# Five per-token rows sent through DRAM, one transposition for the stabiliser, the last token tile in two halves, and another order of the first loads

## The chip, the cores and the metric

The kernel runs on one core of a Trainium2 chip. The metric is the time of one launch on the device in microseconds (us); of several launches the median is given.

## The reference, cut to what matters

One layer of a streaming encoder over 2048 tokens of 1024 features, all in float32:

```python
xn = rms_norm(x, mix_norm_g)
aq, ak, av, mq, mk, mv, mo, i, f, ga, gm = split(xn @ w_in)
A = chunk_band_attention(aq, ak, av, rel_bias)      # chunks of 64 and 8 chunks before them
M = sigmoid(mo) * rms_norm(mlstm_chunkwise(silu(conv(mq, mk)), mv, i, f), mh_norm_g)
y = sigmoid(ga) * (A @ w_att_proj) + sigmoid(gm) * (M @ w_mlstm_proj)
x = x + y @ w_out
x = x + square(relu(rms_norm(x, ffn_norm_g) @ w_up)) @ w_down
return rms_norm(x, final_norm_g)
```

In `mlstm_chunkwise` each token and head has a stabiliser `m_t`, the running maximum that is subtracted before an exponential is taken. Each `rms_norm` needs one factor per token, `(mean of squares + eps) ** -0.5`.

## The kernel before, in words

**Tiles.** The 2048 tokens are four blocks of 512 (`T`). Activations mostly lie with the features on the 128 partitions and 512 tokens along the free side, so a factor per token has to be a row of 512 numbers that is the same on every partition. Where such a factor is computed, it lies the other way round: a tile of 128 partitions by 4 columns, token `t * 128 + p` at partition `p`, column `t`.

**Products.** Every large product is made of float32 tiles that are split in a rounded high part (a copy to fp32r on ScalarE, line 585) and the rest as a low part (a subtraction on VectorE, line 587). Three matmuls with 512 columns replace one: high by high, high by low, low by high. Blocks of 2 by 2 such products are done as seven products of sums, the sums being prepared by VectorE and ScalarE and partly kept in DRAM. Weights come from DRAM on SyncE's queue in tiles of 512 KB into four buffers (`wraw`), split into three (`wsplit`), and TensorE takes them in a fixed sequence.

**The order of the work.** The program first plays through itself in a planner (`Flow`): each step is a generator that yields an engine and a cost in nanoseconds (`yield "pe", 1080`), a wait for an event, or a buffer from a pool. The planner has a clock per engine, adds latencies between engines, lets an event carry the time at which it is set, and gives out the instructions in the order in which they start in its model. A first pass finds how late each step may be, and the second takes the order from these due times. `!` behind an engine's name puts a step first, and `~` marks short float32 work for TensorE. The framework below then schedules anew by priority. On VectorE and ScalarE only the callback `near` (lines 2841 to 2851) binds it: an instruction may not go ahead of those that the planner placed over 10 us (VectorE) or 6 us (ScalarE) earlier. Each engine then works its instructions off in order.

**The places that the change touches.**

- *Start* (`split_first` 553, `loader` 451, `square_in` 1362, `setup` 362). Ten small matmuls run at once (line 370). The first weight tile is loaded in two halves; both are rounded on ScalarE (568) and their rest is taken on VectorE (570). The eight tiles of `x` of block 0 are loaded in turn with the first four weight tiles: events `x_sent` and `w_sent` say which load waits for which in the planner. Each `x` tile is scaled and rounded (1374, ScalarE), its rest taken (1376, VectorE), squared (1383) and summed (1387).
- *Rows* (`rows_far` 1342, `final_scale` 2666). A factor of 128 by 4 becomes a row on all partitions by four matmuls with the identity: the column, repeated 128 times, is the weight. A copy on ScalarE takes the row out of PSUM. `rows_far(0)` does it for blocks 0 and 1, `rows_far(1)` for blocks 2 and 3, and `final_scale` for blocks 0, 1 and 2 at the final norm.
- *Stabiliser* (`gates_rest` 1720). For each of the four blocks the tile `mt` (128 tokens by 16, four groups of tokens times four heads) is turned by four transpositions of 128 by 4, copied out as 4 by 512 and stored to DRAM (`mtd`), from where `load_rec` reads one head's row to all partitions.
- *Last block* (`turned` 2508, `turn_part`, `down_turned` 998, `turned_out` 2562, `turned_put` 2590). The last product of block 3 is made with the tokens on the partitions: four token tiles of 128, each a PSUM bank of 512 features, c = 0 to 3 being the parts of the sum. For c = 3 the tiles are finished one after the other, 12 matmuls each. Behind each tile follow an addition (2570) and a product with the gain (2574) on VectorE, the square with its sum (2586) on ScalarE, a small sum (2577), the power -0.5 on GpSimd (2579), the scaling of two halves of the features (2596, 2599) and two stores, one issued by SyncE (2607) and one by ScalarE (2604). `turned` prepares `eps` times the squared norm of the middle from the row `midd` in DRAM: a square on ScalarE, then four matmuls with a column of ones (2522).

Of the kernel before, what the change touches and what calls it, by code (L numbers as in the profile page):

```python
# [26 lines left out]
ALU = mybir.AluOpType  # L27

P = 128
# [103 lines left out]
class Flow:  # L133
# [32 lines left out]

    def set(self, ev):
        ev.at = self.now
        ev.by = tuple(self.cur.by)
# [144 lines left out]
class Layer:  # L314
    LATE, LANDED = 4000.0, 10000.0

    def __init__(self, nc, pool, psum, io, due=None):
        self.nc, self.io = nc, io
        self.fl = Flow(due)
        self.make_tiles(pool, psum)  # L320
# [130 lines left out]
    def loader(self):  # L451
        fl, io = self.fl, self.io
        i = 0
        for kind, n in self.weights():
# [98 lines left out]
    def split_first(self, src, raw, sent):  # L553

        fl, nc = self.fl, self.nc
        w = yield from self.slot_w(0)
        self.wtile[0] = w
        evs = [Event(), Event()]
        for k, ev in enumerate(evs):
            yield "sp", 800, 2000  # L560
            nc.sync.dma_start(raw[:, k * 512:k * 512 + 512], src[:, k * 512:k * 512 + 512])
            fl.set(ev)
# [435 lines left out]
    def down_turned(self, s, m, ring, A, aev):  # L998
# [3 lines left out]
        for c in range(4):  # L1002
            ws = []
            steps = [(kk, t) for kk in range(2) for t in range(NT)]
            for kk, t in steps if c < 3 else sorted(steps, key=lambda x: x[1]):
# [4 lines left out]
                wv = ws[kk].rearrange("p a (q k n) -> p a k q n", q=2, k=2)  # L1010
                ps = bank[t].rearrange("p (q n) -> p q n", q=2)
                for k in range(2):
                    yield "wait", [aev[m, c][2 * kk + k]]
                    yield "pe", 681
                    a = A[m, c, 2 * kk + k][:, :, t * P:(t + 1) * P]
                    for x, y in ((0, 0), (1, 0), (0, 1)):
                        mm(ps, a[:, y], wv[:, x, k], start=c == kk == k == x == y == 0,  # L1017
                           stop=c == 3 and kk == k == y == 1)
                if kk == 1 and c == 3:
                    fl.spawn(self.turned_out(t, bank[t]), 1)  # L1020
                if t == NT - 1 and c < 3:
                    fl.put(self.wsplit, ws[kk])
            fl.put(ring, *[A[m, c, k] for k in range(4)])

# [317 lines left out]
    def rows_far(self, s, ready, read):  # L1342
# [4 lines left out]
        for b in range(2):  # L1347
            yield "wait", [self.ev_r[2 * s + b]]
            (bk,) = yield "get", self.banks, 1
            yield "pe", 1080  # L1350
# [9 lines left out]
        fl.put(self.bias, *got)  # L1360

    def square_in(self, b, k, x, tot, ev):

        fl, nc = self.fl, self.nc
        dst, g = self.blk[b]["xg"][k], self.gcol[:, 0, k:k + 1]
        if b == 0 and k > 0:
            yield "wait", [self.w_sent[(k - 1) // 2]]
        yield "sp", 800, 2000
        nc.sync.dma_start(x[:, :T], self.io["xt"][b, k])
        if b == 0:  # L1370
            fl.set(self.x_sent[k])
        yield "wait", [self.ev_gain]
# [347 lines left out]
    def gates_rest(self, b, bk):  # L1720
# [82 lines left out]
        V.tensor_scalar(ex[:, 2], ex[:, 2], C1, None, op0=ALU.mult)  # L1803
        yield "pe~", 428
        for c in range(NT):
            nc.tensor.transpose(bk[:MH, c * P:(c + 1) * P], sm["mt"][:, c * MH:(c + 1) * MH], self.ident)
        (tmp,) = yield "get", self.temp, 1
        yield "act", act_ns(512, True)
        nc.scalar.copy(tmp[:MH, :512], bk[:MH])
        fl.put(self.banks, bk)  # L1810
        fl.set(B["gates"])
        fl.spawn(self.store(self.mtd.ap()[b], tmp[:MH, :512], B["rows"], self.temp, tmp), 1)

# [666 lines left out]
    def final(self, s):  # L2480
        fl = self.fl
        tot, mid = yield "get", self.bias, 2
        fl.spawn(self.turned(s, mid), 2)
        summed, ready, sent = [Event() for _ in range(KT + 1)], Event(), []
# [22 lines left out]

    def turned(self, s, mid):

# [5 lines left out]
        for o in range(2):  # L2515
            nc.sync.dma_start(self.tgain[o], self.io["grow"][:, o * 512:o * 512 + 512].to_broadcast([P, 512]))
        ev = Event()
        yield from self.final_mid(2 * s + 1, mid[:, :512], ev)
        (bk,) = yield "get", self.banks, 1
        yield "pe~", 900  # L2520
        for t in range(NT):
            nc.tensor.matmul(bk[:, 2 * t:2 * t + 2], mid[:, t * P:(t + 1) * P], self.ones, start=True, stop=True)
        r, sums = self.rr["z3"], self.rq
        yield "dve", 150
        V.tensor_scalar(r, bk[:, :2 * NT].rearrange("p (t a) -> p t a", a=2)[:, :, 0], 1.0 / D, None, op0=ALU.mult)
        fl.put(self.banks, bk)
        fl.put(self.bias, mid)
        done = [Event() for _ in range(2 * NT)]
# [33 lines left out]
    def turned_out(self, t, ps):  # L2562
# [16 lines left out]
        nc.gpsimd.tensor_tensor(r, r, self.half[:, :1], op=ALU.pow)  # L2579
        fl.spawn(self.turned_put(t, 1, r), 1)  # L2580
        fl.spawn(self.turned_put(t, 0, r), 1)

    def turned_square(self, ps, sums, ev):
        (sq,) = yield "get", self.temp, 1
        yield "act", act_ns(512, True, 1)
        self.nc.scalar.activation(sq[:, :512], ps, AF.Square, accum_out=sums)
        self.fl.put(self.temp, sq)
        self.fl.set(ev)

    def turned_put(self, t, o, r):  # L2590

        nc = self.nc
        x = self.tout[t, o]
        if o or t < NT - 1:
            yield "act", act_ns(512, False, 1)
            nc.scalar.mul(x, x, r)
        else:
            yield "dve", dve_ns(512)
# [67 lines left out]
    def final_scale(self, s, h, slot, summed, ready):  # L2666
# [12 lines left out]
        nc.gpsimd.tensor_tensor(r, r, self.half, op=ALU.pow)  # L2679
        (bk,) = yield "get", self.banks, 1  # L2680
        yield "pe~", 1080
        for t in range(NT):
            nc.tensor.matmul(bk[:, t * P:(t + 1) * P], r[:, t:t + 1].to_broadcast([P, P]), self.ident,
                             start=True, stop=True)
        yield "act", act_ns(512, True)
        nc.scalar.copy(slot[:, :512], bk)
        fl.put(self.banks, bk)
        fl.set(ready)
# [13 lines left out]
    def build(self):  # L2702
# [15 lines left out]
        self.gated, self.mtd = f32d("gatepart", 40, T), f32d("mrow", NB, MH, T)  # L2718
        self.rbd = f32d("relrow", AH, 512)
        self.fin_ev = [E(KT) for _ in range(2)]  # L2720
        self.fin = [f32d(f"fin{h}", KT, P, T) for h in range(2)]
# [139 lines left out]
```

## Time and profile before

| | us |
|---|---|
| median of 3 runs | 2727.39 (2727.08 to 2732.34) |
| span of the profiled execution, first to last instruction | 2725.8 |
| TensorE busy in it | 2708.3 (99%), 12784 matmul records |
| VectorE busy | 2108.8 (77%) |
| ScalarE busy | 1542.1 (57%) |
| GpSimd busy | 48.0 (2%) |

The span is the only time that the profile gives for its own execution; the median lies 1.6 us above it. Each float32 matmul with the identity or with ones leaves two records, a transposition and an fp32r matmul leave one. "PE" is the matmul side of TensorE and "PEld" its weight loads. The rows of a timeline read: start, how long the merged run lasted, engine, line, operation, output and inputs, shapes, how many; in brackets the engine's idle time before it and what ended that.

### The profile page before, as it was taken

Reading aid. Unit: us, or ns where it says so; the run is one execution under the profiler, and the core shown is the slowest. Engines: PE = TensorE matmul, PEld = TensorE weight load, DVE = VectorE, ACT = ScalarE, POOL = GpSimd, SP = SyncE. Lnnn points to the kernel's source line nnn. Section 1 sums busy time; section 2 is a strip of 40 time slices with the busy share of each in tenths; the row PEclk is TensorE's granted clock in tenths of the full one; section 3 lists DMA queues with packets and bytes.
Section 4 is the critical chain, followed back from the end, with each engine's and each line's share of the span. In section 5 each row is a group of like instructions: output and inputs, shape, how many; then the busy total and the mean of one; then the engine's idle time right before and its main releaser. Section 6 shows DMA issues by size and latency. Waiting matters only on the chain.

```text
span 2725.8 us, 38104 instructions
## 1 busy us (share of the span) xinstructions
PE 2708.3 (99%) x12784; PEld 2253.3 (83%) x12784; DVE 2108.8 (77%) x3750; ACT 1542.1 (57%) x2685; POOL 48.0 (2%) x79
## 2 busy tenths in 40 slices
PE   9999999999999999999999999999999999999998
PEld 8878888888888887888888888888888888888887
DVE  7878876888877879987768888889798665657675
ACT  6545456776753645566556766656345565554443
POOL 0000000000000000000000000000000000000000
PEclk9999999999999999999999999999999999999999
DMA  8777889888877889867779787776864454578773
GB/s 305 275 258 277 301 286 293 272 242 275 262 234 238 270 302 321 286 214 265 266 236 288 244 257 225 240 232 220 276 227 160 163 197 159 189 271 285 274 239 134
DMA packets 336712, 678.29 MB, mean 249 GB/s; under 512 B 37396, under 2 KB 66708, under 8 KB 336516
## 3 DMA queue, kind: packets, MB, share of 16 engines
q1 hardware_dynamic: 335796, 674.80, 74.1%
q8 instruction: 100, 1.64, 0.3%
q10 hardware_dynamic: 720, 1.06, 0.1%
q14 instruction: 96, 0.79, 0.1%
HBM read 458.27 MB, written 214.30 MB: 247 GB/s over the span
## 4 chain that ended last, share of the span: by engine, by line
PE 86%; DVE 7%; DMA 3%; issue 2%; ACT 2%; SPq 0%; POOL 0%; ACTq 0%; POOLq 0%; DVEq 0%
PE bank L715 34%; PE bank L746 11%; PE bank L647 8%; PE bank L648 8%; PE bank L646 8%; PE bank L1181 3%; PE bank L751 2%; PE bank L1550 2%; PE bank L1625 2%; PE bank L1657 2%; DVE wsp L587 1%; PE bank L1017 1%; DMA tmp<-in_x 1%; DMA x<-ctx 1%; PE bank L1885 0%
## 5 line engine op out<-in xcount | busy, mean ns | idle before, releaser
L715 PE MATMUL bank<-r,wsp 128*128 128x512 f32 x4872 | 1111.3, 390 | 2.2 <-DVE ctx L2086 1.1
L715 PEld LDWEIGHTS bank<-r,wsp 128*128 128x128 f32 x4872 | 913.0, 188 | 195.0 <-DVE ctx L2086 3.5
L585 ACT CAST wsp<-wraw 128x1024 fp32r<-128x1024 f32 x437 | 459.1, 1051 | 491.4 <-PE bank L715 167.8
L587 DVE TENSOR_TENSOR wsp<-wraw,wsp 128x1024 fp32r<-128x1024 f32 x437 | 534.0, 1222 | 239.0 <-ACT wsp L585 233.7
L646 PE MATMUL bank<-r,wsp 128*128 128x512 f32 x960 | 379.3, 395 | 0.0
L648 PE MATMUL bank<-r,wsp 128*128 128x512 f32 x960 | 375.3, 391 | 0.0
L647 PE MATMUL bank<-r,wsp 128*128 128x512 f32 x960 | 375.2, 391 | 0.0
L746 PE MATMUL bank<-r,wsp 128*128 128x512 f32 x1512 | 368.6, 394 | 0.9 <-DVE ctx L941 0.7
L746 PEld LDWEIGHTS bank<-r,wsp 128*128 128x128 f32 x1512 | 279.0, 188 | 56.9 <-DVE ctx L941 1.6
L648 PEld LDWEIGHTS bank<-r,wsp 128*128 128x128 f32 x960 | 180.2, 188 | 38.5
L647 PEld LDWEIGHTS bank<-r,wsp 128*128 128x128 f32 x960 | 180.5, 188 | 33.4
L646 PEld LDWEIGHTS bank<-r,wsp 128*128 128x128 f32 x960 | 180.4, 188 | 33.5
L1398 DVE TENSOR_TENSOR r<-r 128x512 fp32r<-128x512 f32 x255 | 167.9, 684 | 20.6 <-ACT r L1393 20.0
L2086 DVE TENSOR_TENSOR ctx<-bank,ctx 128x512 f32<-128x512 f32 x174 | 118.9, 686 | 70.3 <-PE bank L715 67.5
L1393 ACT CAST r<-r 128x512 fp32r<-128x512 f32 x255 | 148.8, 617 | 33.4 <-DMA r<-u 30.4
L604 DVE TENSOR_TENSOR wraw<-wraw,wraw 128x1024 f32<-128x1024 f32 x112 | 136.4, 1218 | 4.3 <-DMA wsum<-wraw 3.3
L1638 ACT ACTIVATE sc<-sc,scs 128x640 f32<-128x640 f32 (+4 forms) x128 | 97.6, 763 | 67.5 <-DVE scs L1631 66.5
L2078 ACT COPY ctx<-bank 128x512 f32<-128x512 f32 x174 | 100.9, 583 | 61.0 <-PE bank L715 43.4
L2407 ACT ACTIVATE ctx<-ctx 128x512 f32<-128x512 f32 x96 | 60.6, 631 | 103.2 <-DVE ctx L2086 103.1
L1662 DVE TENSOR_TENSOR r<-bank,r 128x512 fp32r<-128x512 f32 (+1 forms) x168 | 95.7, 593 | 15.0 <-ACT r L1660 14.4
L1550 PE MATMUL bank<-r,r 128*128 128x512 f32 x336 | 94.8, 364 | 0.0
L1660 ACT CAST r<-bank 128x512 fp32r<-128x512 f32 (+1 forms) x168 | 81.0, 516 | 17.2 <-PE bank L1657 16.0
(267 smaller groups left out, 3253.3 us busy)
## 6 DMA issues: line engine op xcount, KB each, us to landing
wraw<-in_wf SPq DMA_DIRECT2D x196, 512.0 KB, 4.9
r<-u SPq DMA_DIRECT2D x224, 256.0 KB, 4.3
wraw<-wsum SPq DMA_DIRECT2D x104, 512.0 KB, 4.6
u<-ctx SPq DMA_DIRECT2D x128, 256.0 KB, 2.4
ctx<-in_wf SPq DMA_DIRECT2D x104, 256.0 KB, 4.4
wsum<-ctx SPq DMA_DIRECT2D x104, 256.0 KB, 4.2
u<-tmp SPq DMA_DIRECT2D x96, 256.0 KB, 2.7
ctx<-in_xt SPq DMA_DIRECT2D x64, 256.0 KB, 4.8
```

What stands on the lines that cost most here:

```text
L585: nc.scalar.copy(w[:, 0], raw)
L587: nc.vector.tensor_sub(w[:, 1], raw, w[:, 0].bitcast(F32))
L604: V.tensor_sub(dst, x, y)
L646: mm(ps, lh, rh, start=first, stop=False)
L647: mm(ps, lh, rl, start=False, stop=False)
L648: mm(ps, ll, rh, start=False, stop=last)
L715: mm(ps, wv[:, x, k, n], a[:, y], start=new and k == 0 and x == y == 0, stop=k == 3 and x == 1, skip_group_check=True)
L746: mm(ps, wv[:, x, k, n], a[:, y], start=start and x == y == 0, stop=stop and x == 1, skip_group_check=True)
L1393: self.nc.scalar.copy(dst[:, 0], src)
L1398: self.nc.vector.tensor_sub(dst[:, 1], src, dst[:, 0].bitcast(F32))
L1550: nc.tensor.matmul(bkv[:, :, c0:c0 + w], st, sl[:, :, o:o + w], start=n == 0, stop=n == total - 1)
L2086: nc.vector.tensor_add(t[:, o:o + 512], ps, t[:, o:o + 512])
```

## The change

Rows: `rows_far(1)` and `final_scale` (five rows in all) store the factor of 128 by 4 to a row of 512 in DRAM, wait for that store, and read the row back to all 128 partitions. `rows_far(0)` stays. `turned` reads one row of `midd` as 128 by 4 and squares it on VectorE, in place of the whole tile, its square and the matmuls.

Stabiliser: one transposition of 128 by 16, one copy of 16 by 128, and a store that puts the 16 rows in place.

Last token tile: for c = 3 the fourth tile is made in two halves of 256 features, 24 matmuls, each half followed by its own addition, square and product. For the other three tiles the product with the gain and the scaling become one VectorE instruction that reads PSUM; the third tile's waits until the fourth's sum is there.

Start: the first half of the first weight tile is rounded on VectorE. The weight tiles are let in one `x` tile earlier, `x` tile `k` now waits for `w_sent[k // 2]`, and some events carry other times. For the planner's first 12 us, and from c = 3 of the last product on (`strict`), VectorE and ScalarE follow the planner's order exactly.

```diff
-    def set(self, ev):
-        ev.at = self.now
+    def set(self, ev, early=0.0):
+        ev.at = (self.now[0] - early, self.now[1])
...
-                yield "wait", [self.x_sent[2 * i]]
+                yield "wait", [self.x_sent[max(0, 2 * i - 1)]]
...
         if sent is not None:
-            self.fl.set(sent)
+            self.fl.set(sent, 2000)
...
         for k in range(2):
             c = slice(k * 512, k * 512 + 512)
             yield "wait", [evs[k]]
-            yield "act", act_ns(512)
-            nc.scalar.copy(w[:, 0, c], raw[:, c])
+            if k == 0:
+                yield "dve!", dve2_ns(512)
+                nc.vector.tensor_copy(w[:, 0, c], raw[:, c])
+            else:
+                yield "act", act_ns(512)
+                nc.scalar.copy(w[:, 0, c], raw[:, c])
...
+            if c == 3:
+                self.strict = True
+                half, self.last_ev = Event(), Event()
+                for q in range(2):
+                    for kk in range(2):
+                        for k in range(2):
+                            yield "pe", 341
...
+                            for x, y in ((0, 0), (1, 0), (0, 1)):
+                                mm(bank[-1][:, q * 256:q * 256 + 256], a[:, y], wv[:, x, k, q], start=False,
+                                   stop=kk == k == y == 1, skip_group_check=True)
+                    fl.spawn(self.turned_half(q, bank[-1], half), 1)
...
+            if s == 1:
+                yield from self.row_of(self.rin[2 + b], self.rowd.ap()[b:b + 1], got[b][:, :T])
+                self.rows[b] = got[b][:, :T]
+                continue
...
+    def row_of(self, r, row, to):
+        kept = Event()
+        yield from self.store(row.rearrange("o (t p) -> p (o t)", p=P), r, kept)
+        yield "wait", [kept]
+        yield "sp", 800, 2500
+        self.nc.sync.dma_start(to, row.to_broadcast([P, T]))
...
         if b == 0 and k > 0:
-            yield "wait", [self.w_sent[(k - 1) // 2]]
-        yield "sp", 800, 2000
+            yield "wait", [self.w_sent[k // 2], self.x_sent[k - 1]]
+        land = 2000 if b else 2650
+        yield "sp", 800, land
...
-        yield "pe~", 428
-        for c in range(NT):
-            nc.tensor.transpose(bk[:MH, c * P:(c + 1) * P], sm["mt"][:, c * MH:(c + 1) * MH], self.ident)
+        yield "pe~", 107
+        nc.tensor.transpose(bk[:16, 0:P], sm["mt"], self.ident)
...
-        ev = Event()
-        yield from self.final_mid(2 * s + 1, mid[:, :512], ev)
-        (bk,) = yield "get", self.banks, 1
-        yield "pe~", 900
-        for t in range(NT):
-            nc.tensor.matmul(bk[:, 2 * t:2 * t + 2], mid[:, t * P:(t + 1) * P], self.ones, start=True, stop=True)
...
+        nc.sync.dma_start(r, self.midd.ap()[2 * s + 1, 0].rearrange("(t p) -> p t", p=P))
         yield "dve", 150
+        V.scalar_tensor_tensor(r, r, EPS, r, op0=ALU.mult, op1=ALU.mult)
...
-        yield "dve", dve_ns(512)
-        V.tensor_mul(low, ps, self.tgain[0])
         yield "wait", [ev]
...
+    def turned_half(self, q, ps, half):
...
+        yield "dve!", dve_ns(256)
+        V.tensor_add(ps, ps, low)
+        ev = Event()
+        fl.spawn(self.turned_square(ps, sums, ev), 1)
+        yield "dve", dve_ns(256)
+        V.tensor_mul(low, ps, self.tgain[0][:, c])
...
+        fl.set(self.last_ev)
...
-        yield "act", act_ns(512, True, 1)
+        n = ps.shape[-1] if not isinstance(ps, Blank) else 512
+        yield "act!", act_ns(512, True, 1)
...
+        elif ps is not None:
+            if t == NT - 2:
+                yield "wait", [self.last_ev]
+            yield "dve", dve_ns(574)
+            nc.vector.scalar_tensor_tensor(x, ps, r, self.tgain[0], op0=ALU.mult, op1=ALU.mult)
...
-        (bk,) = yield "get", self.banks, 1
-        yield "pe~", 1080
-        for t in range(NT):
-            nc.tensor.matmul(bk[:, t * P:(t + 1) * P], r[:, t:t + 1].to_broadcast([P, P]), self.ident,
-                             start=True, stop=True)
-        yield "act", act_ns(512, True)
-        nc.scalar.copy(slot[:, :512], bk)
-        fl.put(self.banks, bk)
+        n = 2 + 2 * s + h
+        yield from self.row_of(r, self.rowd.ap()[n:n + 1], slot[:, :512])
...
-                while len(p) > 1 and p[1][0] <= now - ahead[ins.engine]:
+                back = 0.0 if layer.strict or now < 12000 else ahead[ins.engine]
+                while len(p) > 1 and p[1][0] <= now - back:
```

More of the change, by code (lines that the diff above doesn't have):

```diff
@@ L318, in __init__ @@
         self.nc, self.io = nc, io
-        self.fl = Flow(due)
+        self.fl, self.strict = Flow(due), False
         self.make_tiles(pool, psum)
@@ L1011, in down_turned @@
                 ps = bank[t].rearrange("p (q n) -> p q n", q=2)
+                if c == 3 and t == NT - 1:
+                    continue
                 for k in range(2):
@@ L1017, in down_turned @@
                         mm(ps, a[:, y], wv[:, x, k], start=c == kk == k == x == y == 0,
-                           stop=c == 3 and kk == k == y == 1)
+                           stop=c == (2 if t == NT - 1 else 3) and kk == k == y == 1, skip_group_check=True)
                 if kk == 1 and c == 3:
@@ L2481, in final @@
         fl = self.fl
-        tot, mid = yield "get", self.bias, 2
-        fl.spawn(self.turned(s, mid), 2)
+        (tot,) = yield "get", self.bias, 1
+        fl.spawn(self.turned(s), 2)
         summed, ready, sent = [Event() for _ in range(KT + 1)], Event(), []
@@ L2506, in final1, with turned @@
         fl.set(summed[j])
-    def turned(self, s, mid):
+    def turned(self, s):
         fl, nc = self.fl, self.nc
@@ L2719, in build @@
         self.rbd = f32d("relrow", AH, 512)
+        self.rowd = f32d("tokrow", 5, T)
         self.fin_ev = [E(KT) for _ in range(2)]
@@ L2845, in near @@
                 now = layer.fl.now[0]
-                while len(p) > 1 and p[1][0] <= now - ahead[ins.engine]:
+                back = 0.0 if layer.strict or now < 12000 else ahead[ins.engine]
+                while len(p) > 1 and p[1][0] <= now - back:
                     p.popleft()
-                if p and p[0][0] <= now - ahead[ins.engine]:
+                if p and p[0][0] <= now - back:
                     tc.add_manual_dep(ins, p[0][1], mybir.DependencyInfo(
```

43 lines of the change are left out of this document (31 added, 12 removed).

## The prediction, made before the changed kernel was run

> **What bounds the kernel now.** First the head of the page, its line of engines and its chain; then the view by stretches, cut at 13 us and at 2717.5 us, where TensorE's last matmul ends (from left: stretch, its length, PE, PEld, DVE, ACT, POOL, granted clock, DMA share, GB/s).
>
> ```profile
> span 2725.8 us, 38104 instructions
> PE 2708.3 (99%) x12784; PEld 2253.3 (83%) x12784; DVE 2108.8 (77%) x3750; ACT 1542.1 (57%) x2685; POOL 48.0 (2%) x79
> PE 86%; DVE 7%; DMA 3%; issue 2%; ACT 2%; SPq 0%; POOL 0%; ACTq 0%; POOLq 0%; DVEq 0%
> 0.00:13.00 13.00, 11.70 (x48) 10.02 (x49) 6.73 (x11) 9.13 (x14) 0.21 (x4) 1.00 0.84 311
> 2717.50:2725.80 8.30, 0.00 (x0) 0.00 (x0) 2.10 (x5) 3.32 (x7) 1.08 (x2) 0.67 0.50 188
> ```
>
> TensorE is the bound from end to end: of 2725.8 us it is idle for 17.5, of which 8.3 lie behind its last matmul, 1.3 in the first 13 us and 7.9 in all the rest. So three things can be won: matmuls that vanish (each worth its full slot wherever TensorE has none to spare), the tail, and idle places. The view of the waits, for TensorE (total, times, longest), names some of those:
>
> ```profile
> PE bank L1352 <- POOL r_in L1317: 0.7, 1, 0.7
> PE bank L647 <- DVE wsp L587: 0.3, 1, 0.3
> ```
>
> They are single events below a microsecond, not a pattern: they come from where the planner happened to put a thing. The second is at the start, which is edited; the first is in `rows_far(0)`, which stays, so I keep it.
>
> **Matmuls removed.** The timeline of TensorE alone shows what a group costs: from its first start to the next matmul's start.
>
> ```profile
> 2687.17 0.95 PE L2672 MATMUL bank<-ones,bias 128*128 128x2 f32 x8
> 2687.98 5.07 PE L1017 MATMUL bank<-wsp,r 128*128 128x512 f32 x21
> 2692.88 1.05 PE L2683 MATMUL bank<-const,r_z 128*128 128x128 f32 x8
> 2693.69 0.71 PE L1017 MATMUL bank<-wsp,r 128*128 128x512 f32 x2
> L1352 PE MATMUL bank<-const,r_in x32: 271/275/376, 31.3 to 244.6; 128*128 128x128 f32 x32
> L2683 PE MATMUL bank<-const,r_z x24: 271/275/275, 2492.6 to 2693.7; 128*128 128x128 f32 x24
> L2522 PE MATMUL bank<-ones,bias x8: 165/251/251, 2634.1 to 2634.8; 128*128 128x2 f32 x8
> ```
>
> A row (four float32 matmuls, eight records) takes 2693.69 - 2692.88 = 0.81. L2683 has 24 records, three rows, all removed: 2.43. L1352 has 32, four rows, of which `rows_far(1)`'s two go: 1.62. The eight records with ones in `turned` (L2522) have the shape of L2672, 2687.98 - 2687.17 = 0.81, and go. Together 4.86.
>
> The stabiliser, from the same view, and beside it a single transposition of the form that replaces it (128 by 16):
>
> ```profile
> 173.92 0.60 PE L1806 MATMUL bank<-const,g_mt 128*4 128x128 f32 x4
> 174.27 0.71 PE L715 MATMUL bank<-r,wsp 128*128 128x512 f32 x2
> 157.55 0.27 PE L1760 MATMUL bank<-const,g_u 128*16 128x128 f32 x1
> 157.57 0.71 PE L715 MATMUL bank<-r,wsp 128*128 128x512 f32 x2
> L1806 PE MATMUL bank<-const,g_mt x16: 271/272/273, 173.9 to 1722.0; 128*4 128x128 f32 x16
> ```
>
> Four cost 174.27 - 173.92 = 0.35, one costs 0.02: 0.33 less, in each of four blocks (16 records): 1.3. **All matmuls removed: 6.2.** Each stands inside the dense stream of fp32r matmuls, so nothing hides it and the end moves by as much, if the waits elsewhere stay as they are. The copies on ScalarE (57% busy) that go with them I cost at nothing.
>
> **What the rows cost instead.** Each becomes a store, a wait on SyncE for its landing, and a read, six trips with `turned`'s, which only reads. Behind the waiting store and read stand all later loads on SyncE's queue, weights among them. The view of DMA issues (count, KB each, us to landing):
>
> ```profile
> out_x<-ctx SPq DMA_DIRECT2D x12, 256.0 KB, 2.0
> mix<-tmp SPq DMA_DIRECT2D x40, 64.0 KB, 5.0
> 2694.16 1.23 DVE L587 TENSOR_TENSOR wsp<-wraw,wsp 128x1024 fp32r<-128x1024 f32 x1 [4.64 <-ACT wsp L585]
> 2695.30 5.38 DVE L2658 SCALAR_TENSOR_TENSOR ctx<-ctx,gcol,bias 128x512 f32<-128x512 f32 x8
> 2709.45 0.70 DVE L2570 TENSOR_TENSOR bank<-bank,ctx 128x512 f32<-128x512 f32 x1 [7.62 <-PE bank L1017]
> ```
>
> A landing takes 2.0 to 5.0 us, so a trip takes 4 to 10, against 2.4 from L2683's start to L2658's. In the tightest place, the last `final_scale`, the eight L2658 wait for the row, and L587 for the last weights may stand behind them on VectorE; the engine is idle for 7.6 us before L2570, and the trip is at most 10 - 2.4 = 7.6 longer, so the two just meet. On SyncE the weights behind a wait have four raw buffers, and a tile feeds 24 matmuls of 0.23, 5.5 us each, so 3 us on one trip are covered. Low end therefore 0, which I take, a landing on average lying inside that cover; a gain is excluded, as no wait goes. High end, if the planner's 2.0 and 2.5 us to landing are too short by 3.0 and 2.5 and all of it comes through: 5.5 per trip, 27 for five.
>
> **The start.** The chain in order of time (start, us, what), and two rows of the timeline:
>
> ```profile
> 0.96 4.64 PE L370 MATMUL bank<-ones 128*128 128x128 f32 x20 [0.96 <-DVE ones L365]
> 11.62 0.61 PE L646 MATMUL bank<-wsp,r 128*128 128x512 f32 x2
> 9.69 0.63 ACT ctx L1383
> 10.32 0.95 ACT wsp L585
> 11.30 1.24 DVE wsp L587
> 12.58 0.50 PE bank L647
> ```
>
> The opening matmuls keep TensorE until 0.96 + 4.64 = 5.6, so rounding the first half on VectorE, however fast, starts nothing earlier: 0. The second weight tile is what is late: its rounding (10.32) stands behind a square on ScalarE, which nothing urgent needs, its rest ends at 12.54, and L647 could have started at 11.62 + 2 x 0.23 = 12.08. Loaded one `x` tile earlier and ranked by the planner, it should be rounded about 1 us sooner: the stop of 0.5 goes. What is late next is the rest of the fourth `x` tile, due 0.7 later by the same VectorE; so gain 0.5, bounds 0.5 and -0.5 (a stop of one rest, L1376, in its place). I take 0.5.
>
> **The tail.** The timeline from the last matmul's end on:
>
> ```profile
> 2717.53 0.70 DVE L2570 TENSOR_TENSOR bank<-bank,ctx 128x512 f32<-128x512 f32 x1 [1.00 <-PE bank L1017]
> 2717.67 0.60 ACT L2586 ACTIVATE tmp<-bank 128x512 f32<-128x512 f32 x1 [0.47 <-PE bank L1017]
> 2719.83 0.58 ACT L2586 ACTIVATE tmp<-bank 128x512 f32<-128x512 f32 x1
> 2720.53 0.16 DVE L2577 SCALAR_TENSOR_TENSOR r_z<-r_q,r_z 128x1 f32<-128x1 f32 x1 [1.38 <-ACT tmp L2586]
> 2720.77 0.54 POOL L2579 TENSOR_TENSOR r_z<-r_z,half 128x1 f32<-128x1 f32 x1 [1.60 <-DVE r_z L2577]
> 2721.35 0.72 ACT L2596 ACTIVATE sc<-sc,r_z 128x512 f32<-128x512 f32 x1 [0.24 <-POOL r_z L2579]
> 2721.41 1.03 ACTq L2604 DMA_DIRECT2D out_x<-sc x2
> ```
>
> ScalarE is behind: it squares the third tile at 2717.67, when the fourth is already finished, and the fourth's square waits until 2719.83, though its sum was ready at 2717.53 + 0.70 = 2718.23: 1.6 us. Moving one scaling per tile (0.72) to VectorE and dropping the product in front of the square lets ScalarE keep up (square 0.8, scaling 0.7, issue 0.4 against 2.7 per tile). With halves, an addition and a square of half the length save a further 0.3 each. New chain from the last matmul: addition 0.4, square with its sum 0.5, L2577 0.2, L2579 0.6, scaling 0.7, issue 0.4, gaps 0.3: 3.1, against 2722.44 - 2717.50 = 4.9. The third tile's own scaling on ScalarE (0.7) may stand in that way, and its VectorE product is put behind the sum, beside L2579 and the scaling. Gain 1.1 to 1.8; I take 1.6.
>
> The price is 24 matmuls of 256 columns for 12 of 512. The trace has 256-column ones in pairs, and weight loads as dense as they would be here:
>
> ```profile
> 1868.11 0.39 PE L1550 MATMUL bank<-r,r 128*128 128x256 f32 x2
> 1868.34 0.40 PE L646 MATMUL bank<-r,wsp 128*128 128x512 f32 x1
> L1017 PEld LDWEIGHTS bank<-wsp,r 128*128 128x128 f32 x192 | 35.8, 188 | 7.4
> ```
>
> A pair takes 1868.34 - 1868.11 = 0.23, so 24 take 2.76, as 12 of 512 do: 0.1 at most, the value I take. Were each bound by its weight load (188 ns), 24 would take 4.5: 1.8 more. Were no load covered at all, 24 loads of 0.188 would come on top: 4.5 more. The eight L2683 records, each with a full load of its own, follow each other at 0.81 / 8 = 0.10, which speaks for the pair's value. The Trainium skill, "TensorE: Matmul & The Clock Gate" (Part 3, what overlaps), states that a weight load overlaps running matmuls only when it goes to other rows of the array, which would be the last of the three cases; L2683's spacing does not agree with it.
>
> **Sum.** 6.2 + 0.5 + 1.6 - 0.1 = 8.2 from the span of 2725.8: 2717.6. The median stands 1.6 above the span, so **2719.2 us**.
>
> **Rivals.** (1) *The order laid anew eats part of it.* Costs and buffers change from the first microsecond on, so the planner gives another order, and the 7.9 us of idle places in the middle are drawn again. For: they are chance events; against: most of the dense sequence is fixed. Half as much again, 4 us, leaves 4 of the 8.2: 2723.2, no difference that can be told. (2) *SyncE's queue stops TensorE.* Loads queued behind the five waits arrive late once the raw weights in hand are used up, which takes a delay over the buffers' slack. Against: reads of freshly stored data exist already, and no wait for weights loaded stands among TensorE's. It makes the kernel slower from 8.2 on; at 5.5 lost per trip, 27 in all, 2746; at 3 per trip, 2734. (3) *The halves pay for their weight loads:* bound by them, 1.8 lost at the end, 2721.0; not covered at all, 4.5 lost, 2723.7; the spacing of L2683 speaks against both, more against the second. (4) *The change does not do what it says:* if the exact order leaves ScalarE's last squares where they are, the tail keeps its time and the result is 2720.8, inside the forecast's range.
>
> **How the numbers follow.** What a measurement of this kernel can tell from no change is about 0.2%, 5.5 us: faster is below 2721.9. Forecast with (4) 0.65, its own range 2716 to 2721.5; (1) 0.21; (2) 0.08, the slower side; (3) 0.06, its two cases 0.03 each, the first faster. So faster 0.68, same 0.24, slower 0.08. The range: down to 2714.5, if the idle places fall by 4 as well, and up to 2726, which takes in (1) and (3) and leaves (2) out.
>
> **What would show it.** Right: TensorE busy near 2702; no L1352 for blocks 2 and 3, no row matmuls in `final_scale`; four single transpositions; no stop near 12 us; 24 halves in 2.8 us; ScalarE squaring each tile as TensorE ends it; about 6.5 us behind the last matmul in place of 8.3. Wrong: TensorE idle in the middle by well over 7.9, above all on weights whose loads SyncE issued late; or halves spaced at 0.19.

## The result, and the profile after

| | us |
|---|---|
| changed kernel, median of 5 runs | 2754.17 (2751.83 to 2758.25) |
| kernel before, median of 5 runs beside it | 2730.89 (2727.08 to 2732.78) |
| ratio, 95% interval | 1.0087 (1.0076 to 1.0099) |
| span of the profiled execution | 2752.4 (before 2725.8) |

The change makes the kernel slower by 0.87%, where 0.3% faster was forecast. The head of the changed kernel's page, the chain's shares and the count of DMA packets:

```profile
span 2752.4 us, 38006 instructions
PE 2710.4 (98%) x12736; PEld 2250.0 (82%) x12736; DVE 2113.6 (77%) x3753; ACT 1536.8 (56%) x2678; POOL 46.1 (2%) x79
DMA packets 340504, 679.35 MB, mean 247 GB/s; under 512 B 40628, under 2 KB 70004, under 8 KB 340308
PE 66%; DVE 5%; DMA 3%; issue 3%; ACT 1%; POOL 0%; SPq 0%; POOLq 0%; DVEq 0%; ACTq 0%
```

The matmuls are gone as planned: 60 records went and 12 came with the halves, 12784 - 12736 = 48. Yet TensorE is busy for 2.1 us more, not 6.2 less, and it carries 66% of the last chain where it carried 86%. The same stretches as before, and one early stretch (columns as in the prediction), first of the changed kernel:

```profile
0.00:13.00 13.00, 11.93 (x51) 9.59 (x52) 6.43 (x12) 8.26 (x13) 0.20 (x4) 1.00 0.85 309
13.00:2680.00 2667.00, 2638.46 (x12405) 2191.08 (x12404) 2066.89 (x3680) 1503.14 (x2625) 41.83 (x70) 1.00 0.76 249
2680.00:2745.90 65.90, 60.00 (x284) 49.34 (x282) 38.23 (x60) 23.63 (x38) 3.57 (x4) 1.00 0.41 141
2745.90:2752.40 6.50, 0.00 (x0) 0.00 (x0) 2.04 (x5) 1.81 (x4) 0.54 (x1) 0.50 0.43 161
180.00:300.00 120.00, 107.37 (x455) 87.19 (x454) 82.75 (x122) 53.19 (x85) 2.92 (x2) 0.96 0.77 244
```

and of the kernel before:

```profile
13.00:2680.00 2667.00, 2659.12 (x12558) 2212.09 (x12557) 2083.63 (x3711) 1518.84 (x2648) 43.59 (x70) 1.00 0.75 251
180.00:300.00 120.00, 118.77 (x530) 97.95 (x530) 96.55 (x142) 59.45 (x92) 4.38 (x2) 1.00 0.83 291
```

From 13 to 2680 us TensorE is idle for 2667.00 - 2638.46 = 28.5 us instead of 7.9. Between 2680 us and its last matmul it is idle for another 5.9, where before it was idle for nothing. Behind the last matmul it is idle for 1.8 less, as meant. That is 20.6 + 5.9 - 1.8 = 24.7 of the 26.6; the first 13 us take 0.2 off, and 2.1 are the longer busy time. Of the 28.5 us, 12.6 lie in one place: from 180 to 300 us, where it was 1.2 before. The granted clock (the share of TensorE's full speed that it was given) fell there from 1.00 to 0.96.

The three largest of TensorE's waits in the changed kernel (total, times, longest; of the others none is over 2.1 us), then the timeline around the first stops and near the end:

```profile
PE bank L719 <- DVE ctx L2117: 9.4, 2, 7.6
PE bank L1023 <- DVE wsp L591: 4.3, 2, 2.8
PE bank L719 <- ACT ctx L2109: 3.2, 1, 3.2
```

```profile
205.29 1.23 DVE L608 TENSOR_TENSOR wraw<-wraw,wraw 128x1024 f32<-128x1024 f32 x1 [11.39 <-DMA wsum<-wraw]
210.01 12.64 PE L719 MATMUL bank<-r,wsp 128*128 128x512 f32 x48 [3.24 <-ACT ctx L2109]
272.15 0.69 DVE L522 TENSOR_TENSOR ctx<-ctx,ctx 128x512 f32<-128x512 f32 x1 [9.34 <-DMA ctx<-in_wf]
2726.31 2.08 DVE L2714 SCALAR_TENSOR_TENSOR ctx<-ctx,gcol,bias 128x512 f32<-128x512 f32 x3 [15.04 <-DMA bias<-tokrow]
2734.03 6.88 PE L1023 MATMUL bank<-wsp,r 128*128 128x512 f32 x29 [2.79 <-DVE wsp L591]
2740.74 1.95 PE L1039 MATMUL bank<-wsp,r 128*128 128x256 f32 x15
2743.22 0.62 PE L1039 MATMUL bank<-wsp,r 128*128 128x256 f32 x3 [0.52 <-DVE bank L2616]
2744.86 0.97 PE L1039 MATMUL bank<-wsp,r 128*128 128x256 f32 x6 [1.02 <-DVE ctx L2620]
```

TensorE waits for VectorE (once for ScalarE), and shortly before each of these stops VectorE waited for a DMA: for 11.39 us on `wsum<-wraw`, for 9.34 on `ctx<-in_wf`, for 15.04 on the last row. The first of these was not issued late. It is one of two transfers that were issued at 188.7 and 189.9, and of the two the one whose landing can be told took 15.2 us; in the kernel before the median of such transfers (the row with their count and size) is 3.6:

```profile
L603 SPq DMA_DIRECT2D wsum<-wraw x2: 382/728/1073, 188.7 to 189.9; - x2
DMA to landing us min/median/max: 15.2/15.2/15.2
...
wsum<-wraw SPq DMA_DIRECT2D x32, 512.0 KB, 3.6
```

A stop also costs more than itself: behind the stop of 3.24, 48 matmuls took 12.64 us, where 48 at the pace of an undisturbed run (102 in 23.28 us, kernel 10) take 11.0, so 1.7 us more. The stretches behind this stop and behind the next one, of 1.74 us, show the granted clock (third figure from the right):

```profile
210.00:213.00 3.00, 2.99 (x7) 2.41 (x8) 3.00 (x7) 2.05 (x3) 0.00 (x0) 0.50 0.76 261
213.00:222.60 9.60, 9.60 (x42) 7.58 (x41) 8.11 (x15) 6.19 (x11) 0.00 (x0) 0.99 0.96 339
224.40:228.00 3.60, 3.59 (x14) 2.65 (x15) 3.60 (x6) 2.91 (x6) 0.00 (x0) 1.00 0.47 184
```

The Trainium skill, "TensorE: Matmul & The Clock Gate" (Part 1), states that after an idle window of about 3.4 us the array runs at half its clock for about as long; the 0.50 over 3 us agrees, though the stop here was 3.24 us.

Where do the late landings begin? The view of one tile, `tokrow`, gives the five stores and the five reads (line, count, duration in ns, first and last start), and its last line the time to landing of the one that it can tell, a store:

```profile
L2362 SPq DMA_DIRECT2D tokrow<-r_in x2: 377/412/448, 187.3 to 254.2; - x2
L2362 SPq DMA_DIRECT2D tokrow<-r_z x3: 370/383/385, 2515.9 to 2712.1; - x3
L1390 SPq DMA_DIRECT2D bias<-tokrow x3: 319/319/320, 197.0 to 2721.8; - x3
L1390 SPq DMA_DIRECT2D sc<-tokrow x2: 319/320/320, 2526.1 to 2614.4; - x2
DMA to landing us min/median/max: 10.2/10.2/10.2
```

The first store is issued at 187.3 and its read at 197.0; the last at 2712.1 and 2721.8. The read waits for the store, so a store lands after some 10 us, though it moves 2 KB. It writes a row of 512 tokens from a tile of 128 by 4, one number of 4 bytes at a time. The page shows such short packets too: those under 512 bytes went from 37396 to 40628.

### The profile page after: what moved, and what is told of

It is laid out like the page before. It is cut to its first block, busy times and chain, and to the rows that moved or that the text cites. A ratio compares the mean times of both kernels' runs of the same rounds, so it can differ in the third digit from the quotient of the medians.

```text
span 2752.4 us, 38006 instructions
## 1 busy us (share of the span) xinstructions
PE 2710.4 (98%) x12736; PEld 2250.0 (82%) x12736; DVE 2113.6 (77%) x3753; ACT 1536.8 (56%) x2678; POOL 46.1 (2%) x79
## 4 chain that ended last, share of the span: by engine, by line
PE 66%; DVE 5%; DMA 3%; issue 3%; ACT 1%; POOL 0%; SPq 0%; POOLq 0%; DVEq 0%; ACTq 0%
PE bank L719 27%; PE bank L750 8%; PE bank L650 7%; PE bank L652 7%; PE bank L651 7%; PE bank L1200 2%; PE bank L1581 2%; PE bank L755 2%; PE bank L1656 1%; PE bank L1688 1%; DVE wsp L591 1%; DVE sc L1662 1%; DVE r L1429 0%; DMA tmp<-gate 0%; PE bank L1931 0%
## 5 line engine op out<-in xcount | busy, mean ns | idle before, releaser
L591 DVE TENSOR_TENSOR wsp<-wraw,wsp 128x1024 fp32r<-128x1024 f32 x437 | 533.5, 1221 | 211.8 <-ACT wsp L589 208.7
```

What stands on the lines that cost most here:

```text
L591: nc.vector.tensor_sub(w[:, 1], raw, w[:, 0].bitcast(F32))
```

## The experiments

The first theory (A in the expectations): the rows' trips are the loss, as a store of single numbers lands after 10 us and its wait on SyncE makes what stands behind it late. The rivals: the order laid anew, not the rows; and the halves with their additions. After kernels 6 and 7 stood another form of the first (D): not the wait but the store itself, which holds up every transfer behind it whoever waits. All ratios are to the kernel before, on the same chip.

| kernel | median | ratio, 95% interval | span |
|---|---|---|---|
| 1, changed, rows by TensorE | 2729.93 | 0.9996 (0.9986 to 1.0005) | 2727.8 |
| 2, before, rows by DRAM | 2753.60 | 1.0078 (1.0056 to 1.0099) | 2745.3 |
| 3, changed, rows turned first | 2723.37 | 0.9969 (0.9957 to 0.9981) | 2721.1 |
| 4, as 3, no halves | 2721.96 | 0.9960 (0.9945 to 0.9974) | 2720.6 |
| 5, as 3, halves in two banks | 2720.89 | 0.9969 (0.9958 to 0.9980) | 2719.8 |
| 6, changed, rows by GpSimd's queue | 2759.50 | 1.0112 (1.0095 to 1.0129) | 2758.8 |
| 7, changed, planner told 10 us | 2750.26 | 1.0078 (1.0063 to 1.0093) | 2749.4 |
| 8, before, stabiliser only | 2733.70 | 1.0021 (1.0011 to 1.0030) | 2731.1 |
| 9, before, idle stores of single numbers | 2747.14 | 1.0067 (1.0051 to 1.0084) | 2750.9 |
| 10, before, idle stores of runs | 2728.04 | 0.9998 (0.9988 to 1.0007) | 2727.4 |
| 11, before, the late edits of 5 only | 2723.13 | 0.9985 (0.9976 to 0.9995) | 2725.5 |
| 12, as 5, four transpositions | 2724.05 | 0.9986 (0.9976 to 0.9995) | 2720.9 |

### 1 and 2: everything but the rows, and the rows alone

In kernel 1 the five rows of the changed kernel are made by TensorE again:

```diff
-        n = 2 + 2 * s + h
-        yield from self.row_of(r, self.rowd.ap()[n:n + 1], slot[:, :512])
+        (bk,) = yield "get", self.banks, 1
+        yield "pe~", 1080
+        for t in range(NT):
+            nc.tensor.matmul(bk[:, t * P:(t + 1) * P], r[:, t:t + 1].to_broadcast([P, P]), self.ident,
+                             start=True, stop=True)
...
```

and the same in `rows_far(1)`. Kernel 2 is the kernel before with these two places, and nothing else, as in the change.

> The changed kernel with the five rows made by TensorE again, all else as changed. Theory A (the store of 512 single numbers lands only after some 10 us, SyncE waits for it in front of all later loads, and TensorE stops 3.2 and 7.6 us near 210 and 273 us and 4.3 us near 2730, with its clock low for about 2 us behind each of the two long stops): those stops go, some 20 us, and 4.0 us of row matmuls come back, about 2738. Theory B (the order was laid anew and the stops are chance places of the new order): they stay or turn up elsewhere, about 2758.

> The kernel before with only the five rows by DRAM, the store of 512 single numbers included. Theory A: 4.0 us of matmuls go, stops of about 20 us behind the waits of SyncE come, about 2747, with loads behind each read back issued some 10 us late. Theory B: no such stops, about 2727.

Measured: without the rows by DRAM the loss is gone (0.9996); with them alone it is there (1.0078). From 180 to 300 us, kernel 1:

```profile
180.00:300.00 120.00, 119.97 (x538) 99.28 (x537) 96.41 (x139) 59.30 (x92) 1.45 (x1) 1.00 0.83 292
```

TensorE has no stop there. In kernel 2 it has, as its waits show:

```profile
PE bank L715 <- DVE ctx L2097: 14.6, 3, 7.1
```

The loss belongs to the five rows. Theory A's number for kernel 1, 2738, was 8 us too high and its 2747 for kernel 2 was 7 too low: the rows cost more than the stops that it had counted. Kernel 1 still isn't the 4 us faster that its other edits were costed at; kernel 8 comes back to that.

### 3: the same trips, written in runs

The factor is first turned from 128 by 4 to 4 by 128, so that the store writes four runs of 512 bytes; the store's wait and the read stay as they are:

```diff
+        (bk,) = yield "get", self.banks, 1
+        yield "pe~", 107
+        self.nc.tensor.transpose(bk[:NT, :P], r, self.ident)
+        yield "act", act_ns(128, True)
+        self.nc.scalar.copy(to[:NT, :P], bk[:NT, :P])
+        self.fl.put(self.banks, bk)
-        yield from self.store(row.rearrange("o (t p) -> p (o t)", p=P), r, kept)
+        yield from self.store(row.rearrange("o (t p) -> (o t) p", p=P), to[:NT, :P], kept)
```

> The changed kernel with the factor first turned by one transposition to 4 by 128, copied to SBUF and stored as four runs of 512 bytes; SyncE waits and reads back as before. Theory A (it is the single numbers that make the landing long): store to read back 2 to 5 us in place of 10, the stops near 210, 273 and 2730 gone or below 2 us together, about 2734. Rival A2 (any wait of SyncE for a landing, whatever its pattern, holds the queue long enough): still near 2750. Theory B: no change but chance.

Measured: 0.9969, faster than the kernel before, and 2723.37 where theory A had 2734. The tile `tokrow` in kernel 3, and the early stretch:

```profile
L2368 SPq DMA_DIRECT2D tokrow<-bias x3: 261/261/266, 191.0 to 2687.7; - x3
L1396 SPq DMA_DIRECT2D bias<-tokrow x3: 326/384/1081, 194.4 to 2688.9; - x3
180.00:300.00 120.00, 120.00 (x532) 99.20 (x531) 95.20 (x137) 58.77 (x93) 1.44 (x1) 1.00 0.83 290
```

The last trip's read goes out 2688.9 - 2687.7 = 1.2 us behind its store, the first's 3.4 us, where the changed kernel took 9.7 both times. (The second trip's goes out 8.6 us behind, at 248.9, though its store had landed after 1.8.) So the trip by DRAM is no loss; the pattern of its store is. Kernel 3 changes the length of the runs (4 to 512 bytes), their number (512 to 4) and the partitions that are read (128 to 4) together; no run separates these. The transposition costs TensorE next to nothing: the last one starts at 2687.06 and the next matmul at 2687.09.

### 4 and 5: the last tile

Kernel 4 is kernel 3 with the last token tile in one piece again, the exact order kept. Kernel 5 keeps the halves, but each in a PSUM bank of its own; the sum up to c = 2 is taken out beforehand, into the addend:

```diff
-                                mm(bank[-1][:, q * 256:q * 256 + 256], a[:, y], wv[:, x, k, q], start=False,
+                                mm(two[q][:, q * 256:q * 256 + 256], a[:, y], wv[:, x, k, q], start=kk == k == x == y == 0,
...
+        low = self.tout[NT - 1, 0]
+        self.nc.vector.tensor_add(low, ps, low)
```

> The kernel with the turned rows, and the last token tile in one piece of 512 features again, its order kept exact from there on. Theory C (the second half's matmuls wait until VectorE and ScalarE have read the first half, as both lie in one PSUM bank, 1.5 to 2 us of stops): TensorE's last matmul 1.5 to 2 us earlier, the work behind it about 0.8 us longer, so about 1 us faster than the kernel with the turned rows. Rival: the halves save their 0.6 to 0.8 us, and without them it is that much slower.

> The kernel with the turned rows, and the two halves of the last token tile in two PSUM banks: the sum of the parts c = 0 to 2 is added to the lower half of the features beforehand, and each half of part c = 3 starts a bank of its own. Theory C (one shared bank makes the second half's matmuls wait 0.5 and 1.0 us): no stop among the 24 matmuls, which take 2.8 us in place of about 4.9, the work behind them unchanged at about 6.6 us, so 1.5 to 2 us off the 2723.4 of the kernel with the turned rows. Rival (the stops come from something else, VectorE being late): they stay, no change.

Measured: 0.9960 and 0.9969, not to be told from each other or from kernel 3's 0.9969. The traces can tell: TensorE's timeline at the end of kernel 5, and its stretch from there on:

```profile
2704.76 5.60 PE L1023 MATMUL bank<-wsp,r 128*128 128x512 f32 x24
2710.20 3.03 PE L1044 MATMUL bank<-wsp,r 128*128 128x256 f32 x24
2713.30:2719.80 6.50, 0.00 (x0) 0.00 (x0) 2.04 (x6) 1.81 (x4) 1.08 (x2) 0.70 0.44 164
```

With two banks the 24 halves run through in 3.0 us. In the changed kernel they take from 2740.74 to 2745.83, 5.1 us: the second half's matmuls wait while VectorE adds to the first half of the same bank (L2616) and reads it (L2620). With one piece 7.3 us lie behind the last matmul, with halves 6.6. So halving wins 0.7 and the shared bank costs 2 (5.1 - 3.0), by these traces; the times can't tell.

### 6 and 7: is it SyncE's wait, or the planner's 2 us?

In kernel 6 the store and the read of the changed kernel go by GpSimd's queue, on which nothing else waits; in kernel 7 the planner is told that the store lands after 10 us:

```diff
+        yield "pool", 800, 2000
+        self.nc.gpsimd.dma_start(row.rearrange("o (t p) -> p (o t)", p=P), r)
```

```diff
+        yield "sp", 800, 10000
+        self.nc.sync.dma_start(row.rearrange("o (t p) -> p (o t)", p=P), r)
```

> The changed kernel with the store of 512 single numbers and its read moved from SyncE's queue to GpSimd's, which has little else to do. Theory A, its second half (TensorE stops because SyncE holds the loads behind the wait): the store still takes about 10 us to its read, no stop of over 2 us near 210 and 273 us, about 2735 to 2740, since VectorE still waits for the last row near 2720. Rival (the consumers of the row themselves are late, whoever waits): stops as long as in the changed kernel, about 2754.

> The changed kernel with the planner told that the store of single numbers lands after 10 us, not 2. If the planner's price is what makes SyncE wait in front of loads that it could have issued first, other loads move in between store and read, the stops near 210, 273 and 2730 shrink, and the time is about 2735. If the scheduling behind the planner or the order of the queue decides, the stops stay and so does the time, about 2754.

Measured: 1.0112 and 1.0078, neither faster than the change by more than 0.1%. The stops stay in kernel 6 although SyncE no longer waits for the store: the first line is TensorE's longest wait there. The view of tile `qfar` shows why: first the transfers issued up to 184 us, then the one issued at 186.2, after the store at 185.0 on the other queue:

```profile
PE bank L719 <- DVE ctx L2119: 10.9, 3, 6.8
...
L2364 SPq DMA_DIRECT2D qfar<-ctx x3: 319/319/320, 177.9 to 181.6; - x3
L2364 SPq DMA_DIRECT2D qfar<-tmp x2: 319/352/384, 179.2 to 181.0; - x2
DMA to landing us min/median/max: 2.1/2.7/3.0
...
L2364 SPq DMA_DIRECT2D qfar<-ctx x1: 319/319/319, 186.2 to 186.2; - x1
DMA to landing us min/median/max: 10.4/10.4/10.4
```

The same kind of transfer, 256 KB, lands after 2.7 us ahead of the store and after 10.4 behind it. So the half of theory A that put the loss on SyncE's wait fell, and the store itself came under suspicion. Kernel 7 says that the planner's belief is not it either: the order changes, the stops move (2.3 us ahead of 207, 5.8 ahead of 225), and the loss stays.

### 9 and 10: stores for which nobody waits

The kernel before, its rows by TensorE as ever, with five stores added that nothing reads and nothing waits for; the planner does not know of them. Kernel 9 writes single numbers, kernel 10 four runs of 512 bytes from a constant:

```diff
+                self.nc.sync.dma_start(self.rowd.ap()[b:b+1].rearrange("o (t p) -> p (o t)", p=P), self.rin[2 + b])
```

```diff
+                self.nc.sync.dma_start(self.rowd.ap()[b:b+1].rearrange("o (t p) -> (o t) p", p=P), self.const[:NT, 0])
```

> The kernel before, computing its rows on TensorE as before, with five stores of 512 single numbers added at the places of the rows, for which nobody waits and which nobody reads; the planner does not know of them, so its order is that of before. Theory D (the store itself holds up the DMA engines for some 10 us, and every transfer behind it lands that much later, so engines that wait for loads stop): stops of 2 to 7 us near 200 and 255 us, 8 to 20 us slower, 2738 to 2750. Theory A (only a wait of SyncE for the landing, or of the rows' users, costs anything): no change, 2730.

> The same five added stores at the same places with as many bytes, but as four runs of 512 bytes from four partitions. Theory D: they land in 2 to 5 us, no stop, no change from before, 2730. If an added store of any pattern disturbs the queue or the order: as slow as the single numbers.

Measured: 1.0067 and 0.9998. Kernel 9's first store goes out at 180.8; `qfar` in the next four microseconds, and in the kernel before at the same time; then the early stretch, a late one, and TensorE's two longest waits in kernel 9:

```profile
L1350 SPq DMA_DIRECT2D tokrow<-r_in x2: 370/370/371, 180.8 to 242.2; - x2
...
L2333 SPq DMA_DIRECT2D qfar<-ctx x2: 319/319/319, 182.3 to 184.3; - x2
L2333 SPq DMA_DIRECT2D qfar<-tmp x2: 382/392/401, 182.7 to 183.2; - x2
DMA to landing us min/median/max: 9.9/10.0/10.2
...
L2331 SPq DMA_DIRECT2D qfar<-tmp x1: 320/320/320, 183.4 to 183.4; - x1
DMA to landing us min/median/max: 2.0/2.0/2.0
...
180.00:300.00 120.00, 111.16 (x481) 90.95 (x480) 86.58 (x126) 54.89 (x87) 3.93 (x2) 0.96 0.89 256
2100.00:2680.00 580.00, 570.92 (x2539) 471.04 (x2538) 379.41 (x491) 303.88 (x460) 2.41 (x2) 1.00 0.61 211
...
PE bank L715 <- DVE ctx L2088: 7.9, 3, 5.4
PE bank L648 <- DVE wsp L587: 6.5, 4, 2.4
```

Nobody waits for these stores, and yet the four transfers of `qfar` right behind the first take 10 us where one took 2.0 before, TensorE is idle for 8.8 us in the early stretch, and the kernel loses 0.67%, 18 us (14 to 23). Not all of it is lost where the changed kernel loses: TensorE is idle here for 9.1 us from 2100 to 2680, where the changed kernel has none. The DMA engines count as busier in that stretch (0.89 against 0.83) and yet move less, 256 GB/s instead of 291. So theory D holds, as far as these transfers show. Kernel 10 is a weaker control than meant: its constant does not depend on the factor, so its first two stores went out at 118.7 and 119.0, not at the rows' places. At those places kernel 3 is the control.

### 8, 11 and 12: what the order laid anew does

Kernel 8 is the kernel before with the single transposition of the stabiliser and its store, nothing else. Kernel 11 is the kernel before with kernel 5's `final_scale`, `turned` and tail; its start, `rows_far` and stabiliser are the old ones. Kernel 12 is kernel 5 with the four old transpositions.

```diff
-        yield "pe~", 428
-        for c in range(NT):
-            nc.tensor.transpose(bk[:MH, c * P:(c + 1) * P], sm["mt"][:, c * MH:(c + 1) * MH], self.ident)
+        yield "pe~", 107
+        nc.tensor.transpose(bk[:16, 0:P], sm["mt"], self.ident)
```

This is kernel 8's edit and, taken back, kernel 12's. Kernel 11 has from kernel 5, beside the tail, this in `final_scale`, with `row_of` as in kernel 3, and `turned`:

```diff
+        yield from self.row_of(r, self.rowd.ap()[n:n + 1], slot[:, :512])
...
+        nc.sync.dma_start(r, self.midd.ap()[2 * s + 1, 0].rearrange("(t p) -> p t", p=P))
```

> The kernel before with only the stabiliser's single transposition. By the removed slots alone 1.3 us faster, no difference that can be measured. It also shows how much a small edit moves the idle places in the middle of the trace: theory B holds that TensorE's idle time between 13 and 2680 us differs by some us from the 7.9 of before; if the order is stable, it stays within 1 us.

> The kernel before with only late edits: the last norm's three rows turned and stored in runs, the row of the middle read as 128 by 4, and the end of the changed kernel with its halves in two banks. By slots: 2.4 - 0.2 + 0.8 - 0.1 of TensorE's time and 1.6 behind its last matmul, 4.5 us. Theory B (any edit lays the whole order anew through the due times, and the idle places of before are a lucky draw): the idle time between 13 and 2400 us moves by some us, and the gain is blurred. If the order ahead of 2400 us stays as it was: 4 to 5 us faster, about 2726.

> The kernel with turned rows and two banks, with the stabiliser's four transpositions as before. By slots 1.3 us slower than with one transposition, 2722. Theory B: within 5 us of that either way, since the idle places in the middle are drawn again.

Measured: kernel 8 is slower than the kernel before by 0.21% (0.11 to 0.30), although 1.3 us of matmuls went. Its long stretch:

```profile
13.00:2680.00 2667.00, 2655.11 (x12523) 2208.47 (x12522) 2081.70 (x3703) 1514.47 (x2643) 42.90 (x70) 1.00 0.75 251
```

TensorE is idle there for 11.9 us instead of 7.9, at lines such as L751 and L1550, which are not the stabiliser's. In kernel 12, on the other hand, taking the same edit back costs 1.1 us of span, as its matmuls say. So the one edit seems to have both signs, which points to the order that the planner happens to lay out. It is not shown: the edit also stores `mtd` in 16 runs of 512 bytes instead of four of 2 KB, and the second sign is as small as what these runs can tell. Kernel 11 was to gain 4.5 us by its matmuls and tail; it gains 0.15% (0.05 to 0.24), 4 us, though its profiled span is 0.3 below the kernel before's. Kernel 12 measures 0.9986 against kernel 5's 0.9969, 3 us apart in the medians and 1.1 in the spans. Differences of 3 us are the limit of what these runs settle, and why a given order stops TensorE where it does stays open.

## Why the prediction was wrong

**The step that failed** is the one headed "What the rows cost instead", and in it the sentence "Low end therefore 0, which I take, a landing on average lying inside that cover". The landing of 2.0 to 5.0 us came from rows of 64 and 256 KB transfers, whole rows of numbers (the same view has reads of 256 KB at up to 6.2 us, `r<-qfar`). The stores of the change have another pattern, and neither of those rows is near it: 512 writes of 4 bytes land after 8.3 to 11.4 us (kernel 6's five stores). And the cost was looked for in the wrong place. The step asked who waits for the store on SyncE; kernel 9 shows a loss with no one waiting, with transfers behind the store that land about 10 us after issue. A cover of 3 us on one trip or four raw buffers is no match for that. The "high end" of 27 us, made of other causes, is near what was paid: the changed kernel lies 32 us (1.0087 - 0.9969 = 0.0118) above kernel 3, which differs in how that store is written; that includes the half pace behind stops and an order laid anew. Kernel 9's stores alone cost 18 (14 to 23), in part in other places; the rest has no experiment of its own. VectorE's 15 us for the last row and TensorE's 4.3 us behind it on L591 are of the rest, as nobody waits for a row in kernel 9.

**The rivals.** Rival (2), given 0.08, had the right sign and nearly the size (2734 to 2746 against 2754.17). Its mechanism, loads issued late behind SyncE's waits, is not what was measured: kernel 6 frees SyncE and keeps the loss. That its size is near is luck. Rival (1) has something in it: kernel 8 is idle in the middle for 4 us more on an edit that was to gain 1.3. Kernel 1 stands at 0.9996 where slots, start and tail promised about 4 us; it is idle in the middle for 2.3 us more than the kernel before, and for 1.55 at the shared bank. Such shifts make single terms of 1 us hard to find again. Rival (3) fell: 15 halves ran in 1.95 us, 0.13 each, not 0.19. Rival (4) fell with the changed tail.

**Matmuls removed, 6.2:** the records went as counted. The busy time of 2710.4 is 8.4 above the 2702 that was named as a sign. Part of that is the half pace behind stops, 1.7 us at one place. Kernel 3, without those stops, is busy for 2701.6 us.

**The start, 0.5:** the stop at 12.58 is gone; up to 40 us only the opening matmuls' own wait is left. At 13 us TensorE has worked 11.93 instead of 11.70; in kernel 3, which has the same edits, it has worked 11.49. What of it reaches the end can't be told apart from the redrawn order.

**The tail, 1.6:** 6.5 us lie behind the last matmul instead of 8.3, as forecast. **The halves, 0.1** was mis-sized: 5.1 us for 24, 2.2 more than said. Weight loads are not the cause (kernel 5's take 191 ns each and its halves 0.13 us) but the shared bank, which the prediction did not look at; kernel 5 takes that away.

**The sum.** With the store in runs the forecast's size is met: kernel 3 gains 0.31% (0.19 to 0.43), and 8.2 of 2727.39 is 0.30%. That is luck in part. Kernel 3's profiled span is only 4.7 us below that of the kernel before (one execution each): 6.7 less busy time and 1.7 less behind the last matmul, against 2.0 more idle time in the middle, 1.5 at the shared bank and 0.2 in the first 13 us. Kernels 4 and 5 beat both the kernel before and the changed one, at 0.9960 (0.9945 to 0.9974) and 0.9969 (0.9958 to 0.9980).

## What to carry to other kernels

Price a transfer by its pattern, not by its bytes: look in the trace for a row that writes as short runs as the new one, and where there is none, turn the data on chip first, so that runs of hundreds of bytes go out. When transfers land late though they were issued in time, look for what was issued just ahead of them on any queue, not for who waits. An edit that makes a planner lay out its order anew can move some microseconds by itself, as kernel 8's 4 us of idle time suggest, so terms smaller than that are to be tried in more than one setting before they are believed.

## What the runs showed of the hardware

- A store of 512 single 4-byte numbers took 8.3 to 11.4 us to land (kernel 6's five), a store of the same 2 KB in four runs of 512 bytes 1.2 to 3.9 (kernel 3's five, by the semaphore updates in its trace). Reading single numbers is no such matter: `turned`'s read of 512 of them landed after 4.9 us in kernel 1, and after 4.6 in kernel 3, between neighbours that took 3.0 and 4.8. The Trainium skill, "DMA: Bandwidth & Descriptors" (Specifications), states that below 512 bytes the engine does a read-modify-write; that the writes are slow and the reads not agrees with it, but no run here shows the read-modify-write itself. Why the engines do not take other transfers in between was not tried.
- The store holds up transfers of another queue too: behind it on GpSimd's queue, a 256 KB transfer on SyncE's took 10.4 us, where those ahead of it took 2.7 (kernel 6).
- Behind a stop of 3.24 us the granted clock was 0.50 for 3 us, which cost 1.7 us more; behind one of 1.74 us it stayed at 1.00 (changed kernel).
- Weight loads that the trace gives as 191 ns each did not hold matmuls of 256 columns to that spacing: 24 of them took 3.03 us, 0.13 each (kernel 5).
